# One loop over both halves' queries, and a regrouped top-k selection, in a two-layer decoder trunk on one core

## The chip, the cores and the metric

The kernel runs on one core of a Trainium2 chip. That core has five engines with a program of their own each: TensorE (PE in the rows: matmuls, with PEld for its weight loads), VectorE (DVE), ScalarE (ACT), GpSimd (POOL) and SyncE (SP, which here issues the DMAs). An engine works through its instructions strictly in order and waits on semaphores for the others. The metric is the device time of one execution. Three runs of the kernel before took 2650.87, 2652.57 and 2655.19 us; the median, 2652.57 us, is the time before.

## The reference, cut to what matters

The reference is a decoder trunk of two layers over 1024 tokens of width 1024. The change is in the first layer, a sparse attention. An indexer scores every key for every query; only the 256 best keys of a query are attended to:

```python
dots  = einsum('bqhd,bsd->bqhs', q_idx, k_idx)            # 16 index heads of 64
score = einsum('bqhs,bqh->bqs', relu(dots), w_idx)
score = where(causal, score, -inf)
_, idx = top_k(score, 256)                                 # per query
s = (q_lat . c_sel + q_rope . kr_sel) * 128 ** -0.5        # on the gathered keys
o_lat = softmax(s) @ c_sel
```

Around it lie the projections of the normed input (`h @ w_in`: queries, latent keys, index queries, memory queries), a cross-attention to a memory of 256 rows, and a gated MLP of width 2816 with a causal convolution. The second layer has windowed attention in place of the sparse one. All of it is in float32.

## The kernel before

**Tiling.** Activations lie with features on the 128 partitions and tokens along the free axis, in two halves of 512 tokens. Every float32 product is made of three matmuls on a high and a low part (`mm3`, lines 256 to 258). So each weight block of 128x1024 is split when it is fetched: a load of 512 KB by SP (line 87), a cast on ACT (line 99) and two subtractions of 512 columns on POOL (line 279). Results come out of PSUM by ACT (high part, line 264) and DVE (low part, line 265). PSUM has two buffers of 1024 columns (`pS`) and four of 512 (`pB`).

**Order of the work.** The program is written by hand in one thread. Long pieces of other work are generators; `tick(ns)` advances a virtual clock at each step of the main line, and a background generator issues its next instructions when the nanoseconds that it asked for with `yield` have passed on that clock. So a generator with more yields is spread over more matmuls, and `finish_bg(b)` issues whatever is left of `b` in one piece.

**The stretch concerned.** For each half, `a_q` multiplies the four pairs of query blocks (11 to 18 of `a_in`) with that half's `h`; so each of these eight weight blocks is fetched and split twice. Beside it run in the background the indexer of token blocks 2 to 7 (`indexer`, PE line 1203, ACT line 1206, DVE lines 1209 and 1211), the selection `topk` of blocks 2 and 3 and, once the scores are there, of blocks 4 to 7, and the cross-attention to the memory (`mem_units`, PE lines 713 and 714, DVE line 715, ACT line 719).

**The selection.** A block holds 128 queries; their scores are up to 1024 columns, (block + 1) x 128. `topk` finds the 256th largest score of each row bit by bit: for each of 32 bits it makes a candidate (`cand`), counts how many scores reach it, and keeps the bit or not. DVE counts with line 1239. For the blocks in `act` (6 and 7) ACT counts instead, as a sum of signs of the score less the candidate (line 1247). In one call all blocks go in step: when the last count of a bit is in, lines 1264, 1265 and 1268 judge it for all blocks at once, line 1261 makes the next candidate, line 1244 its negative for ACT, and the first count of the next bit follows with no yield between. For blocks 2 and 3, without `act`, these are lines 1267, 1268 and 1261, then two counts (384 and 512 columns). At the end lines 1291 to 1304 turn the scores into a mask, with the ties resolved; for a block in `act`, lines 1278 to 1287 first find the exact candidate.

**What waits for it.** Attention of the first half starts from `att = self.attn_a(0)`; its unit 2 is the first whose mask needs blocks 2 and 3, and `att[0][2].before` calls `finish_bg(*bt)` for their selection. The selection of blocks 4 to 7 goes on through that attention and through the MLP of the first half. There the down projection fills `pS` with twelve matmuls at a time and DVE adds it to the residual (line 867); a third use of `pS` waits for that add.

Of the kernel before, what the change touches and what calls it, by code (L numbers as in the profile page):

```python
# [173 lines left out]
class Trunk:  # L174
# [970 lines left out]
    def a_q(self, hf, h, tab):  # L1145
        ts = slice(hf * HT, hf * HT + HT)
        for j in (6, 0, 2, 4):
            def dst(hl, e, j=j + 0):
                at = (j + e) * 16
                return self.q_d[hl, at:at + 16].rearrange("i h t -> (i h) t")[:, ts]  # L1150

            S = self.pair("a_in", 11 + j, h)
            if j == 6:
                self.rope_store("q", S, tab, 0, 1.0, dst)
            else:
                self.store_hl("q", S, dst)
# [61 lines left out]
    def topk(self, blks, pace, act=()):  # L1218
# [6 lines left out]

        nc, nb = self.nc, len(blks)
        wks = [self.work[b][:, :(b + 1) * 128] for b in blks]
        ints = self.sb.tile([128, 6, 4], I32, name="ti", tag="ti", bufs=2)
        found, flip, cand, keep, less, pick = [ints[:, i, :nb] for i in range(6)]
        floats = self.sb.tile([128, 5, 4], F32, name="tc", tag="tc", bufs=2)  # L1230
        cnt, need, reach, low, high = [floats[:, i, :nb] for i in range(5)]
        order = [i for i in range(nb) if blks[i] not in act]
        order[1:1] = [i for i in range(nb) if blks[i] in act]
# [8 lines left out]
        def counts():  # L1242
# [10 lines left out]
        for i, b in enumerate(blks):  # L1253
            nc.vector.memset(need[:, i:i + 1], float(2 * TOPK - 1 - (b + 1) * 128 if b in act else TOPK))
        nc.vector.memset(found, 0)
        nc.vector.memset(cand, 0)
        yield from counts()
        nc.vector.tensor_tensor(reach, cnt, need, op=OP.is_lt)
        nc.vector.tensor_scalar(flip, reach, -1.0, 0.0, op0=OP.mult, op1=OP.add)
        for bit in range(30, -1, -1):  # L1260
            nc.vector.scalar_tensor_tensor(cand, found, 1 << bit, flip, op0=OP.bitwise_or, op1=OP.bitwise_xor)
            yield from counts()
            if act:
                nc.vector.tensor_tensor(reach, cnt, need, op=OP.is_ge)
                nc.vector.tensor_scalar(keep, reach, float(1 << bit), 0.0, op0=OP.mult, op1=OP.add)
            else:
                nc.vector.tensor_scalar(keep, cnt, float(TOPK), float(1 << bit), op0=OP.is_ge, op1=OP.mult)
            nc.vector.tensor_tensor(found, found, keep, op=OP.bitwise_or)
        nc.vector.tensor_tensor(cand, found, flip, op=OP.bitwise_xor)
# [431 lines left out]
    def run(self):  # L1701
# [84 lines left out]
        mem = self.mem_units(0)  # L1786
        tab = self.load_table("q32", 0)
# [354 lines left out]
```

## Time and profile before

| of the profiled execution | |
|---|---|
| its time | 2653.03 us |
| span, first to last instruction | 2651.2 us |
| outside the span | 1.8 us |
| median of the three timed runs | 2652.57 us |
| PE busy | 2472.4 us (93%) |
| DVE busy | 1755.7 us (66%) |
| ACT busy | 1188.9 us (45%) |
| POOL busy | 1419.6 us (54%) |
| mean granted TensorE clock | 0.970 of full speed |

A busy time counts the engine as busy while an instruction of it runs, and also while a running instruction is held up; a share over the whole span is a mean over stages with different limits, so the rows further down are of single stretches. The granted clock is 1 at full speed, and half of that in the slow stretches. The selection of blocks 2 and 3 runs from 177 us to 366 us of the span, that of blocks 4 to 7 from 390 us to 857 us.

### The profile page before, as it was taken

What the parts mean: (1) busy time and instruction counts of PE and PEld (TensorE: products, weight loads), DVE (VectorE), ACT (ScalarE), POOL (GpSimd) and SP (SyncE); (2) the same over time, 40 slices, a digit from 0 to 9 for tenths busy, and PEclk for the clock granted to TensorE, in tenths of its full rate; (3) what the DMA queues carried; (4) which work ended last, traced back from release to release, by engine and by line L of the source; (5) the groups of instructions that cost most, each with busy time, mean ns of one, the idle gap of its engine ahead of it and who ended that gap; (6) DMA issues with size and microseconds to landing.
All of it is one profiled execution on the core that took longest, in us unless ns stands there. A gap on an engine that the chain in (4) does not pass through costs nothing. (4 is left out here: it accounts for less than half of the span.)

```text
span 2651.2 us, 34066 instructions
## 1 busy us (share of the span) xinstructions
PE 2472.4 (93%) x11912; PEld 2061.4 (78%) x11912; DVE 1755.7 (66%) x3016; ACT 1188.9 (45%) x2214; POOL 1419.6 (54%) x1256
## 2 busy tenths in 40 slices
PE   7789889989997999999999989999989999999997
PEld 5677668867776889877778878888767888887886
DVE  7899998876779466664663362598786656554446
ACT  5344557644542555433333234678644444441103
POOL 5644344455555643356766655657656565664304
PEclk8899999999998999999999999999999999999999
DMA  5454346422222253332323336543154333348301
GB/s 201 148 172 135 121 135 212 144 72 95 89 80 80 78 189 128 103 106 86 112 81 111 113 84 212 176 159 111 64 182 156 107 112 111 112 160 339 137 23 64
DMA packets 122236, 338.03 MB, mean 127 GB/s; under 512 B 13136, under 2 KB 30032, under 8 KB 122064
## 3 DMA queue, kind: packets, MB, share of 16 engines
q1 hardware_dynamic: 122064, 335.85, 37.5%
q8 instruction: 94, 1.54, 0.2%
q14 instruction: 78, 0.64, 0.1%
HBM read 262.40 MB, written 73.40 MB: 127 GB/s over the span
## 5 line engine op out<-in xcount | busy, mean ns | idle before, releaser
L279 POOL TENSOR_TENSOR t<-t,t 128x512 fp32r<-128x512 f32 (+1 forms) x845 | 1134.1, 1372 | 705.5 <-ACT t L99 274.7
L256 PE MATMUL pB<-t,t 128*128 128x512 f32 (+3 forms) x1824 | 683.1, 374 | 10.6 <-DVE t L781 4.0
L257 PE MATMUL pB<-t,t 128*128 128x512 f32 (+3 forms) x1824 | 679.8, 373 | 9.4 <-DVE t L461 7.4
L258 PE MATMUL pB<-t,t 128*128 128x512 f32 (+3 forms) x1824 | 679.4, 372 | 5.4 <-POOL t L279 5.4
L256 PE MATMUL pS<-t,t 128*128 128x512 f32 (+1 forms) x1460 | 577.1, 395 | 56.4 <-DVE t L867 25.6
L258 PE MATMUL pS<-t,t 128*128 128x512 f32 (+1 forms) x1460 | 571.7, 392 | 9.0 <-POOL t L279 8.8
L257 PE MATMUL pS<-t,t 128*128 128x512 f32 (+1 forms) x1460 | 571.1, 391 | 2.7 <-DVE t L512 2.7
L256 PEld LDWEIGHTS pB<-t,t 128*128 128x128 f32 (+1 forms) x1824 | 346.9, 190 | 71.4 <-DVE t L781 4.8
L257 PEld LDWEIGHTS pB<-t,t 128*128 128x128 f32 (+1 forms) x1824 | 347.0, 190 | 69.3 <-DVE t L461 8.6
L258 PEld LDWEIGHTS pB<-t,t 128*128 128x128 f32 (+1 forms) x1824 | 346.7, 190 | 67.0 <-POOL t L279 6.7
L256 PEld LDWEIGHTS pS<-t,t 128*128 128x128 f32 x1460 | 284.0, 195 | 117.9 <-DVE t L867 35.1
L99 ACT CAST t<-t 128x1024 fp32r<-128x1024 f32 (+1 forms) x292 | 296.9, 1043 | 105.0 <-PE pS L258 49.5
L258 PEld LDWEIGHTS pS<-t,t 128*128 128x128 f32 x1460 | 282.5, 193 | 69.6 <-POOL t L279 13.5
L257 PEld LDWEIGHTS pS<-t,t 128*128 128x128 f32 x1460 | 283.6, 194 | 54.6 <-DVE t L512 3.2
L265 DVE TENSOR_TENSOR t<-pB,t 128x512 fp32r<-128x512 f32 (+3 forms) x248 | 149.7, 622 | 83.4 <-ACT t L264 80.5
L264 ACT CAST t<-pB 128x512 fp32r<-128x512 f32 (+3 forms) x248 | 126.3, 534 | 151.2 <-PE pB L258 88.0
L1055 DVE TENSOR_TENSOR t<-t,pS 128x1024 f32<-128x1024 f32 (+1 forms) x92 | 107.9, 1174 | 125.6 <-PE pS L258 125.4
L867 DVE TENSOR_TENSOR t<-t,pS 128x1024 f32<-128x1024 f32 x88 | 106.4, 1216 | 63.2 <-PE pS L258 63.1
L811 POOL TENSOR_TENSOR t<-t,t 128x512 f32<-128x512 f32 x44 | 57.4, 1304 | 166.8 <-ACT t L810 166.8
L1430 POOL TENSOR_SCALAR t<-t,st 128x128 f32<-128x128 f32 (+3 forms) x64 | 47.8, 749 | 139.5 <-DVE st L1429 79.8
L802 ACT ACTIVATE t<-t,conv 128x512 f32<-128x512 f32 x44 | 35.9, 815 | 171.3 <-DVE t L801 171.3
L1239 DVE TENSOR_SCALAR_CACHE_REDUCE hit<-t,ti 128x384 bf16<-128x384 f32 (+5 forms) x136 | 111.4, 819 | 1.6
(234 smaller groups left out, 3100.1 us busy)
## 6 DMA issues: line engine op xcount, KB each, us to landing
t<-in_up SPq DMA_DIRECT2D x138, 512.0 KB
t<-in_down SPq DMA_DIRECT2D x66, 512.0 KB
G_d<-t SPq DMA_DIRECT2D x44, 512.0 KB
t<-G_d SPq DMA_DIRECT2D x44, 512.0 KB
t<-in_a_in SPq DMA_DIRECT2D x42, 512.0 KB
t<-in_b_in SPq DMA_DIRECT2D x28, 512.0 KB
t<-in_a_out SPq DMA_DIRECT2D x20, 512.0 KB
t<-x_d SPq DMA_DIRECT2D x20, 512.0 KB
```

The costliest lines, as they stand in the source:

```text
L99: nc.scalar.copy(hi[:, :w], raw[:, :w])
L256: mm(out, a[0], b[0], start=start, stop=False, skip_group_check=again)
L257: mm(out, a[0], b[1], start=False, stop=False, skip_group_check=again)
L258: mm(out, a[1], b[0], start=False, stop=stop, skip_group_check=again)
L264: nc.scalar.copy(hi, src)
L265: nc.vector.tensor_tensor(lo, src, hi.bitcast(F32), op=OP.subtract)
L279: self.nc.gpsimd.tensor_tensor(lo[:, s], src[:, s], hi[:, s].bitcast(F32), op=OP.subtract)
L811: nc.gpsimd.tensor_tensor(v, v, rb[0], op=OP.mult)
L867: nc.vector.tensor_tensor(x[dp][:, :, t], x[dp][:, :, t], S, op=OP.add)
L1055: nc.vector.tensor_tensor(xp, xp, S, op=OP.add)
L1239: nc.vector.tensor_scalar(hits("hit")[:, :(blks[i] + 1) * 128], wks[i], cand[:, i:i + 1].bitcast(F32), 0.0, op0=op, op1=OP.add, accum_out= ...
L1430: nc.gpsimd.tensor_scalar(Pt[:, :n], Pt[:, :n], st[:, 2:3], 1.0, op0=OP.mult, op1=OP.mult)
```

## The change

Three things are changed.

First, `a_q` handles both halves in one loop: each pair of query blocks is fetched and split once and multiplied with the first half's `h` and then the second's. The rotation tables are loaded within it, and the memory's cross-attention is put into the background after six of the eight products (`between`), where before it started after four.

Second, the selection of blocks 2 and 3 lets ACT count block 3 (`act=(3,)`).

Third, `topk` keeps no `found`, `flip` and `need` any more: `cand` itself is the number under construction, and one step is two DVE instructions, `drop` (lines 1265 and 1266 of the new file) and the xor into `cand` (line 1267). The step is made apart for the blocks that DVE counts (`own`) and for those that ACT counts, each with a yield behind it; block 6 is counted over 1024 columns, its last 128 filled with -3e38 by POOL.

The two selections get other numbers of yields: a bit of blocks 2 and 3 has three where it had two, a bit of blocks 4 to 7 has four as before.

```diff
-    def a_q(self, hf, h, tab):
+    def a_q(self, hs, between):
+        tabs = [self.load_table("q32", 0)]
         for j in (6, 0, 2, 4):
...
+            us = [self.w.get("a_in", 11 + j + e) for e in range(2)]
+            for hf, h in enumerate(hs):
...
+                for e in range(2):
+                    self.proj(S[:, e], us[e], h)
...
+            if j == 2:
+                between()
...
         def count(i, op):
             nc.vector.tensor_scalar(hits("hit")[:, :(blks[i] + 1) * 128], wks[i], cand[:, i:i + 1].bitcast(F32), 0.0,
                                     op0=op, op1=OP.add, accum_out=cnt[:, i:i + 1])
...
+        def step(bit, part):
+            at, need = part
+            nc.vector.tensor_scalar(drop[:, at], cnt[:, at], float(need), float(1 << bit) if bit < 31 else -1.0,
+                                    op0=OP.is_lt, op1=OP.mult)
+            nc.vector.scalar_tensor_tensor(cand[:, at], drop[:, at], 1 << bit >> 1, cand[:, at],
+                                           op0=OP.bitwise_xor, op1=OP.bitwise_xor)
+
+        for bit in range(31, -1, -1):
+            for k in range(max(len(own), nb - len(own))):
+                if len(own) + k < nb:
+                    i = len(own) + k
+                    nc.scalar.activation(hits("sign")[:, :wide], self.work[blks[i]][:, :wide], AF.Sign,
+                                         bias=cand[:, i:i + 1].bitcast(F32), accum_out=cnt[:, i:i + 1])
+                if k < len(own):
+                    count(k, OP.is_ge)
+                yield pace
+            if own:
+                step(bit, parts[0])
+                yield pace
             if act:
-                nc.vector.tensor_scalar(less, cand, -(1 << 31), None, op0=OP.bitwise_xor)
-            for i in order:
-                if blks[i] in act:
-                    nc.scalar.activation(hits("sign")[:, :(blks[i] + 1) * 128], wks[i], AF.Sign,
-                                         bias=less[:, i:i + 1].bitcast(F32), accum_out=cnt[:, i:i + 1])
-                else:
-                    count(i, OP.is_ge)
+                step(bit, parts[-1])
                 yield pace
...
-        for bit in range(30, -1, -1):
-            nc.vector.scalar_tensor_tensor(cand, found, 1 << bit, flip, op0=OP.bitwise_or, op1=OP.bitwise_xor)
-            yield from counts()
-            if act:
-                nc.vector.tensor_tensor(reach, cnt, need, op=OP.is_ge)
-                nc.vector.tensor_scalar(keep, reach, float(1 << bit), 0.0, op0=OP.mult, op1=OP.add)
-            else:
-                nc.vector.tensor_scalar(keep, cnt, float(TOPK), float(1 << bit), op0=OP.is_ge, op1=OP.mult)
-            nc.vector.tensor_tensor(found, found, keep, op=OP.bitwise_or)
...
-            bt.append(self.add_bg(self.topk((2, 3), 1400)))
+            bt.append(self.add_bg(self.topk((2, 3), 1400, (3,))))
...
-        self.a_q(0, h0, tab)
-        tab = self.load_table("q32", 1)
         bgs.append(self.a_latent(1, h1))
-        bm = self.add_bg(self.whole(mem[0]))
-        self.a_q(1, h1, tab)
+        reads = []
+        self.a_q((h0, h1), lambda: reads.append(self.add_bg(self.whole(mem[0]))))
+        bm = reads[0]
```

By the built programs the change takes away 8 DMAs of `in_a_in` on SP, 8 casts of 128x1024 on ACT and 16 subtractions of 128x512 on POOL, and 31 counts of 512 columns on DVE; it adds 32 counts of 512 columns on ACT and turns 32 of 896 columns into 1024. PE's instructions are the same in number.

What moves is seen in two places. The first is DVE in the MLP's down projection of the first half; L867 is the add to the residual, L1264 to L1244 judge one bit of blocks 4 to 7 and make the next candidate, L1239 counts. Before:

```order
L1264 TENSOR_TENSOR tc<-tc 128x4
L1265 TENSOR_SCALAR ti<-tc 128x4
L1268 TENSOR_TENSOR ti<-ti 128x4
L1261 SCALAR_TENSOR_TENSOR ti<-ti 128x4
L1244 TENSOR_SCALAR ti<-ti 128x4
L1239 TENSOR_SCALAR hit,tc<-t_1918,ti 128x640
L867 TENSOR_TENSOR t_3731<-t_3731,pS 128x1024
L867 TENSOR_TENSOR t_3733<-t_3733,pS 128x1024
```

And now, with L1265 and L1267 the two instructions of a step and L1254 the count:

```order
L867 TENSOR_TENSOR t_3567<-t_3567,pS 128x1024
L1265 TENSOR_SCALAR ti<-tc 128x2
L1267 SCALAR_TENSOR_TENSOR ti<-ti 128x2
L1254 TENSOR_SCALAR hit,tc<-t_1911,ti 128x640
L867 TENSOR_TENSOR t_3569<-t_3569,pS 128x1024
L1254 TENSOR_SCALAR hit,tc<-t_2285,ti 128x768
L867 TENSOR_TENSOR t_3571<-t_3571,pS 128x1024
L1265 TENSOR_SCALAR ti<-tc 128x2
L1267 SCALAR_TENSOR_TENSOR ti<-ti 128x2
L867 TENSOR_TENSOR t_3573<-t_3573,pS 128x1024
```

Where six instructions of the selection stood in one run ahead of an add, runs of one to three now stand between the adds.

The second place is DVE just ahead of attention unit 2 of the first half; L620 and L622 take the second half's memory queries out of PSUM, L265 is the next evacuation that PE needs, and t_1134 and t_1323 are the scores of blocks 2 and 3. Before:

```order
L1244 TENSOR_SCALAR ti<-ti 128x4
L1239 TENSOR_SCALAR hit,tc<-t_1918,ti 128x640
L620 SCALAR_TENSOR_TENSOR t_3723<-pS,t_3723 64x1024
L622 SCALAR_TENSOR_TENSOR t_3724<-pS,t_3724 64x1024
L265 TENSOR_TENSOR t_3743<-pB,t_3743 128x384
L1421 ISA t_3750,st<-pB,t_1134 128x384
```

And now, first the beginning and then the end of what stands between L622 and L265:

```order
L620 SCALAR_TENSOR_TENSOR t_3561<-pS,t_3561 64x1024
L622 SCALAR_TENSOR_TENSOR t_3562<-pS,t_3562 64x1024
L1265 TENSOR_SCALAR ti<-tc 128x1
L1267 SCALAR_TENSOR_TENSOR ti<-ti 128x1
L1254 TENSOR_SCALAR hit,tc<-t_1134,ti 128x384
L1265 TENSOR_SCALAR ti<-tc 128x1
L1267 SCALAR_TENSOR_TENSOR ti<-ti 128x1
```

```order
L1304 TENSOR_TENSOR ti<-ti,tc 128x1
L1254 TENSOR_SCALAR hit,tc<-t_1323,ti 128x512
L1308 TENSOR_SCALAR tc<-tc 128x2
L1313 TENSOR_SCALAR t_3626<-t_1134,ti 128x384
L1315 SCALAR_TENSOR_TENSOR t_3627<-t_3626 128x384
L1317 SCALAR_TENSOR_TENSOR t_3627<-t_3627,tc,t_3626 128x384
L1319 SCALAR_TENSOR_TENSOR t_1134<-t_1134,ti,t_3627 128x384
L1321 TENSOR_SCALAR t_1134<-t_1134 128x384
```

The selection of blocks 2 and 3, which had ended well ahead of this place, is now unfinished there: its last four bits and all that follows them, 47 instructions of DVE and 4 counts of ACT, are issued in one piece between L622 and L265.

## Rows read from the trace of the kernel before

**Rows 1.** Page, part 1: busy us (share of the span) xinstructions, by engine.
```profile
PE 2472.4 (93%) x11912; PEld 2061.4 (78%) x11912; DVE 1755.7 (66%) x3016; ACT 1188.9 (45%) x2214; POOL 1419.6 (54%) x1256
```
**Rows 2.** Busy time by stretch: PE, PEld, DVE, ACT, POOL; clock, DMA share, GB/s.
```profile
165.00:400.00 235.00, 208.83 (x991) 170.79 (x990) 214.13 (x402) 118.83 (x232) 105.03 (x80) 0.96 0.42 138
425.00:550.00 125.00, 117.37 (x650) 100.10 (x649) 103.40 (x264) 75.84 (x158) 55.13 (x57) 0.97 0.45 149
550.00:800.00 250.00, 230.39 (x979) 187.62 (x978) 176.35 (x290) 119.88 (x188) 137.68 (x108) 0.97 0.25 83
```
**Rows 3.** Waits, 165 to 400 us: who for whom, us in total, times, longest.
```profile
PE pB L1203 <- ACT t L719: 13.7, 4, 8.6
...
ACT t L719 <- DVE st L715: 21.3, 6, 9.3
```
**Rows 4.** Waits of PE, 550 to 800 us.
```profile
PE pS L256 <- DVE t L867: 18.0, 6, 6.9
```
**Rows 5.** Timeline of PE: start us, us, instruction, [idle before, releaser].
```profile
599.13 0.79 PE L256 MATMUL pS<-t,t 128*128 128x512 f32 x1 [6.92 <-DVE t L867]
...
603.13 0.63 PE L256 MATMUL pS<-t,t 128*128 128x512 f32 x1
...
604.11 0.39 PE L256 MATMUL pS<-t,t 128*128 128x512 f32 x1
```
**Rows 6.** Timeline of DVE, and POOL beside it, at 668 us.
```profile
668.88 0.15 DVE L1264 TENSOR_TENSOR tc<-tc 128x4 f32<-128x4 f32 x1
669.07 1.17 DVE L1265 TENSOR_SCALAR ti<-tc 128x4 int32<-128x4 f32 x1
...
672.74 1.19 DVE L1244 TENSOR_SCALAR ti<-ti 128x4 int32<-128x4 int32 x1
673.84 0.87 DVE L1239 TENSOR_SCALAR_CACHE_REDUCE hit<-t,ti 128x640 bf16<-128x640 f32 x1
...
667.69 6.21 POOL L279 TENSOR_TENSOR t<-t,t 128x512 fp32r<-128x512 f32 x5 [1.51 <-ACT t L820]
```
**Rows 7.** Groups of DVE by form, selection of blocks 2 and 3: busy us, mean ns.
```profile
L1239 DVE TENSOR_SCALAR_CACHE_REDUCE hit<-t,ti 128x512 bf16<-128x512 f32 x33 | 24.4, 741 | 0.3
L1239 DVE TENSOR_SCALAR_CACHE_REDUCE hit<-t,ti 128x384 bf16<-128x384 f32 x33 | 20.2, 612 | 1.2
L1267 DVE TENSOR_SCALAR ti<-tc 128x2 int32<-128x2 f32 x31 | 18.0, 582 | 0.2
L1268 DVE TENSOR_TENSOR ti<-ti 128x2 int32<-128x2 int32 x31 | 12.4, 400 | 1.1
L1261 DVE SCALAR_TENSOR_TENSOR ti<-ti 128x2 int32<-128x2 int32 x31 | 8.1, 262 | 1.1
```
**Rows 8.** Groups of DVE, 338 to 380 us: the masks of blocks 2 and 3.
```profile
L1302 DVE SCALAR_TENSOR_TENSOR t<-t,ti,t 128x384 f32<-128x384 f32 (+1 forms) x2 | 2.3, 1140 | 0.1
L1298 DVE TENSOR_TENSOR_SCAN t<-t 128x384 f32<-128x384 f32 (+1 forms) x2 | 2.3, 1140 | 0.1
L1304 DVE TENSOR_SCALAR t<-t 128x384 f32<-128x384 f32 (+1 forms) x2 | 1.8, 876 | 0.0
L1300 DVE SCALAR_TENSOR_TENSOR t<-t,tc,t 128x384 f32<-128x384 f32 (+1 forms) x2 | 1.6, 790 | 0.0
L1296 DVE TENSOR_SCALAR t<-t,ti 128x384 f32<-128x384 f32 (+1 forms) x2 | 1.1, 525 | 0.0
```
**Rows 9.** Groups: ACT's count over 1024 columns, and POOL's splits from 165 to 400 us.
```profile
L1247 ACT ACTIVATE sign<-t,ti 128x1024 bf16<-128x1024 f32 x32 | 36.7, 1147 | 0.5
...
L279 POOL TENSOR_TENSOR t<-t,t 128x512 fp32r<-128x512 f32 (+2 forms) x62 | 88.7, 1454 | 115.6 <-ACT t L99 83.2 <-issue 22.2 <-DMA q_d<-t 7.3
```
**Rows 10.** Timelines of DVE and PE at attention unit 2, before.
```profile
405.34 0.17 DVE L1258 TENSOR_TENSOR tc<-tc 128x4 f32<-128x4 f32 x1
405.54 0.17 DVE L1259 TENSOR_SCALAR ti<-tc 128x4 int32<-128x4 f32 x1
...
411.08 0.96 PE L1417 MATMUL pB<-t,t 128*128 128x512 f32 x3 [3.50 <-DVE t L265]
```

More of the change, by code (lines that the diff above doesn't have):

```diff
@@ L1143, in a_latent, with dst @@
         return self.add_bg(latent_norm())
-    def a_q(self, hf, h, tab):
-        ts = slice(hf * HT, hf * HT + HT)
+    def a_q(self, hs, between):
+        tabs = [self.load_table("q32", 0)]
         for j in (6, 0, 2, 4):
[L1148 to L1154, printed above, removed]
-            else:
-                self.store_hl("q", S, dst)
+            us = [self.w.get("a_in", 11 + j + e) for e in range(2)]
+            for hf, h in enumerate(hs):
+                ts = slice(hf * HT, hf * HT + HT)
+                def dst(hl, e, j=j + 0, ts=ts):
+                    at = (j + e) * 16
+                    return self.q_d[hl, at:at + 16].rearrange("i h t -> (i h) t")[:, ts]
+                S = self.psS().rearrange("p (j t) -> p j t", j=2)
+                for e in range(2):
+                    self.proj(S[:, e], us[e], h)
+                if j == 6:
+                    self.rope_store("q", S, tabs[hf], 0, 1.0, dst)
+                    if not hf:
+                        tabs.append(self.load_table("q32", 1))
+                else:
+                    self.store_hl("q", S, dst)
+            if j == 2:
+                between()
     def a_first(self, raw, rb):
@@ L1226, in topk @@
         nc, nb = self.nc, len(blks)
+        own = [b for b in blks if b not in act]
+        blks = own + [b for b in blks if b in act]
         wks = [self.work[b][:, :(b + 1) * 128] for b in blks]
[L1228 to L1233, printed above, removed]
+        ints = self.sb.tile([128, 3, 4], I32, name="ti", tag="ti", bufs=2)
+        cand, drop, pick = [ints[:, i, :nb] for i in range(3)]
+        floats = self.sb.tile([128, 3, 4], F32, name="tc", tag="tc", bufs=2)
+        cnt, low, high = [floats[:, i, :nb] for i in range(3)]
+        wide = (max(act) + 1) * 128 if act else 0
+        parts = [(slice(0, len(own)), TOPK), (slice(len(own), nb), 2 * TOPK - 1 - wide)]
         def hits(tag):
@@ L1240, in count @@
                                     op0=op, op1=OP.add, accum_out=cnt[:, i:i + 1])
-        def counts():
-            if act:
-                nc.vector.tensor_scalar(less, cand, -(1 << 31), None, op0=OP.bitwise_xor)
-            for i in order:
-                if blks[i] in act:
-                    nc.scalar.activation(hits("sign")[:, :(blks[i] + 1) * 128], wks[i], AF.Sign,
-                                         bias=less[:, i:i + 1].bitcast(F32), accum_out=cnt[:, i:i + 1])
-                else:
-                    count(i, OP.is_ge)
-                yield pace
@@ L1253, in topk @@
[L1253 to L1256, printed above, removed]
-        yield from counts()
-        nc.vector.tensor_tensor(reach, cnt, need, op=OP.is_lt)
-        nc.vector.tensor_scalar(flip, reach, -1.0, 0.0, op0=OP.mult, op1=OP.add)
-        for bit in range(30, -1, -1):
-            nc.vector.scalar_tensor_tensor(cand, found, 1 << bit, flip, op0=OP.bitwise_or, op1=OP.bitwise_xor)
-            yield from counts()
-            if act:
-                nc.vector.tensor_tensor(reach, cnt, need, op=OP.is_ge)
-                nc.vector.tensor_scalar(keep, reach, float(1 << bit), 0.0, op0=OP.mult, op1=OP.add)
-            else:
-                nc.vector.tensor_scalar(keep, cnt, float(TOPK), float(1 << bit), op0=OP.is_ge, op1=OP.mult)
-            nc.vector.tensor_tensor(found, found, keep, op=OP.bitwise_or)
@@ L1269, in topk @@
-        nc.vector.tensor_tensor(cand, found, flip, op=OP.bitwise_xor)
+        nc.vector.memset(cand, 0)
+        if act:
+            nc.vector.tensor_scalar(cand[:, len(own):], cand[:, len(own):], -(1 << 31), None, op0=OP.bitwise_xor)
+            for b in act:
+                if (b + 1) * 128 < wide:
+                    nc.gpsimd.memset(self.work[b][:, (b + 1) * 128:wide], -3e38)
+        def step(bit, part):
[4 more added lines that the diff above has]
+                                           op0=OP.bitwise_xor, op1=OP.bitwise_xor)
@@ L1270, in topk @@
+        if act:
+            nc.vector.tensor_scalar(cand[:, len(own):], cand[:, len(own):], -(1 << 31), None, op0=OP.bitwise_xor)
         for i in range(nb):
@@ L1786, in run @@
         mem = self.mem_units(0)
-        tab = self.load_table("q32", 0)
         bgs.append(self.a_latent(1, h1))
-        self.a_q(0, h0, tab)
-        tab = self.load_table("q32", 1)
+        reads = []
+        self.a_q((h0, h1), lambda: reads.append(self.add_bg(self.whole(mem[0]))))
+        bm = reads[0]
         del h0
-        bm = self.add_bg(self.whole(mem[0]))
-        self.a_q(1, h1, tab)
         self.finish_bg(*bgs, be)
@@ L1800, in run @@
         self.store_qmem(self.pair("a_in", 19, h1), 1)
-        del h1, tab
+        del h1
         self.finish_bg(ba)
```

## The prediction, made before the changed kernel had run

> **What bounds the kernel now.** The first view is the page's part 1 [rows 1]: PE is busy 93% of the span, DVE 66%, ACT 45%, POOL 54%. So PE is the bound on the mean, and a change on the other engines can win only what PE loses by waiting for them, or by running at half clock after a wait. The second view is the busy time by stretch [rows 2], to see where that loss lies within the reach of the change. From 165 to 400 us PE is busy 208.83 of 235 us, so it idles 26.2 us; the mean granted clock is 0.96, and 4% of 235 us, 9.4 us, is what the slow clock took. DVE is busy 214.13 us there, 91%, more than PE. From 425 to 550 us (attention) the loss is 7.6 us idle and 3.8 us of clock, from 550 to 800 us (the MLP) 19.6 us and 7.5 us. After the selection's end at 857 us, no instruction is changed.
>
> The third view is who waits for whom. From 165 to 400 us the largest entry has PE waiting 13.7 us for ACT's L719, but ACT's L719 itself waits 21.3 us for DVE's L715 [rows 3]: the late engine is DVE. From 550 to 800 us 18.0 of PE's 19.6 us are six waits for L867, DVE's add to the residual [rows 4]. The timeline shows what such a wait costs in all: after 6.92 us of waiting PE runs its matmuls 0.63 us long until past 603 us, at half of full clock, and 0.39 us long from 604.11 us on [rows 5]. And it shows why DVE is late: at 668.88 us it judges a bit, and four of the five small instructions, on 4 elements per partition, take some 1.2 us each; then a count of 0.87 us follows, and only then an add. POOL is working through five splits from 667.69 us for 6.21 us [rows 6], so the small ones end where POOL's end.
>
> **The change part by part.** All sums are made against the profiled execution: 2653.03 us, of which 2651.2 us are the span. That is 0.5 us above the median of the runs shown.
>
> *Fetching the query weights once.* 8 loads of 512 KB, 8 casts and 16 subtractions go. DMA is busy 42% there and POOL 105.03 of 235 us [rows 2], so neither is on the path, and the direct gain is nothing. Indirectly, 16 x 1.45 us [rows 9] = 23 us of POOL's 105 go, and with them a fifth of the occasions on which DVE is held up; that is in the middle value below.
>
> *Blocks 2 and 3, ahead of attention unit 2.* DVE loses 31 counts of 512 columns: 31 x 0.741 = 23.0 us [rows 7]. A bit had three small instructions and now has four (two steps of two). Those three take 0.582, 0.400 and 0.262 us on the mean [rows 7], 0.415 us each; at that price the 93 before cost 38.6 us. Of the 128 now, 18 lie in the piece ahead of unit 2, and 110 cost 45.6 us: 7.0 us more. The dearest price, 0.582 us for each, gives 25 us more; with 0.17 us, that of an unhindered one [rows 10], it is 20 us less. With three yields per bit in place of two the selection is slower by the virtual clock, and four bits, the last counts and the masks fall out of this stretch: 4 x 0.612, 0.612 + 0.741 and the masks' 2.3 + 2.3 + 1.8 + 1.6 + 1.1 = 9.1 us [rows 7, 8], together 12.9 us. So DVE has 214.1 - 23.0 + 7.0 - 12.9 = 185 us of work ahead of unit 2. PE needs 235 - 35.6 = 199 us without any loss. DVE falls below PE and the backlog can drain. ACT gets 28 counts of 512 columns, each below the 1.147 us of 1024 columns [rows 9]: at most 32 us on 118.83 of 235 [rows 2], room enough.
>
> How much of the 35.6 us comes back no row says directly. The nearest is 425 to 550 us, where DVE is busy 83% and PE loses 11.4 of 125 us, 9% [rows 2]; at that rate 199 us of work take 219 us, a gain of 16. If half the loss goes, the stretch takes 209 us, a gain of 26. I take 20 us. The bounds: nothing (the dearest small instructions put DVE at 203 us, over PE's 199, and ACT's counts now stand in line behind DVE), and 35 us.
>
> *The piece ahead of unit 2.* DVE runs in order, and L265, which empties the PSUM buffer that PE needs next, stands behind the piece. Its length: 24 small instructions at the 0.20 us from start to start of [rows 10] = 4.8 us; 5 counts of 384 columns, 3.1 us; 2 of 512, 1.5 us; for the exact candidate of block 3 two selections at the 0.525 us of L1296 and two reductions, for which the nearest row is the count of the same width, 0.741 us, 2.5 us; the masks 9.1 us [rows 7, 8]. Together 21 us. ACT's four counts run beside DVE's own, and hardly add. PE has two or three microseconds of scores and transposes that need nothing from the piece. The same place costs a wait of 3.50 us already [rows 10], and the piece comes on top: 20 us. After it PE starts at half clock, as in [rows 5]; 6 us of that lose 3 us. So 23 us lost. The bounds are 14 us (the masks at their cheapest, and more of PE's work found ahead) and 45 us (every small instruction at 1.2 us, as in [rows 6]).
>
> Here a rule of the Trainium skill weighs in: SBUF — State Buffer, section SBUF: two separate sides, has it that VectorE and GpSimd share one pair of ports as an exclusive lock, taken for a whole instruction by whichever starts first, and that a VectorE instruction with two SBUF inputs needs the pair. By that, the small ones in the piece cost 0.2 us, since POOL has little left to do when PE stands, where the mean row of 0.415 us would make the piece 5 us longer. The trace agrees where it can: in [rows 6] the small ones stretch as long as POOL's splits run.
>
> *Blocks 4 to 7, in attention and the MLP.* A bit had five small instructions and the first count in one run; now it has two pairs with yields between, and at most a pair and a count meet: 2 x 1.2 + 0.87 us at worst against 4 x 1.2 + 0.87 us in [rows 6]. Two buffers of `pS` give DVE the time of twelve matmuls per add, so most of the six waits go. ACT's count of block 6 grows from 896 to 1024 columns, 0.1 us each, hidden by its idle half. I take 20 us of the 27.1 us lost between 550 and 800 us (15 of the 18.0 us waited for L867, and 5 of the 7.5 us of clock). The bounds are 5 us (the pairs still meet an add badly) and 27 us. In attention PE hardly waits for these steps: 2 us, between 0 and 6. The rest of the MLP, 800 to 900 us, has the masks of blocks 4 to 7 in the same order as before: nothing.
>
> The sum: -20 + 23 - 20 - 2 = -19 us. 2653.03 - 19 = 2634 us.
>
> **The rivals.** *All of the backlog goes.* For it: DVE's 185 us against PE's 199. Against: bursts remain, as in every stretch of [rows 2]. 30 us gained ahead of unit 2, 18 lost at the piece, 25 and 4 gained after: 2612 us.
>
> *ACT is tied to DVE.* Before, ACT evacuated the indexer's scores whether or not DVE's selection was late. Now a count of ACT stands ahead of these evacuations and waits for DVE's step of the same bit. For it: DVE is late ahead of unit 2 [rows 3]. Against: the step is issued a yield earlier. If that eats the 20 us, the sum is +1: 2654 us.
>
> *The waits for L867 stay.* If they come from POOL's splits more than from the length of the run, one pair held up twice is enough: 5 gained in place of 20, a sum of -4: 2649 us. Against: four held instructions made the run of [rows 6], and two are the most now.
>
> *The piece ahead of unit 2 decides: slower.* Its price is that of DVE in order, with PE behind it. If POOL still has splits and the memory's scalings in that time, and the small ones cost 1.2 us, the piece is 45 us; with 3 us of clock, and 16 gained ahead, 17 after and 1 in attention, the sum is +14: 2667 us. It decides from about 42 us on, what the other terms give together. Against: PE stands, so POOL runs dry.
>
> **How the numbers follow.** My forecast, 2622 to 2646 us, has a chance of 0.58; all of the backlog 0.14; ACT tied to DVE 0.11; the waits stay 0.07; the piece decides 0.10. Faster or slower means by over 0.2% of the median, below 2647.3 or above 2657.9 us, about what a measurement can tell. Faster: 0.58 + 0.14 and a third of the two middle rivals, together 0.76. Same: most of the rest of these, 0.13. Slower: 0.11. The range from 2611 to 2656 us takes in both sides up to the two middle rivals, and leaves out the slower one and the far end of the faster.
>
> **What would show each step.** Right: from 165 us to unit 2, DVE's busy share falls below PE's, and PE's wait for L719 shrinks; one wait of PE of some 20 us stands ahead of unit 2, released by L265 on DVE; between 550 and 800 us waits for L867 come to under 5 us, and the clock there is 0.99. Wrong: DVE still at 90% or more ahead of unit 2; ACT waiting long for the selection's steps with PE behind it; no wait of over 10 us at unit 2; or six waits for L867 as before. The whole is wrong if the time lies above 2656 us.

## The result and the profile after

The changed kernel takes 2624.34 us (median of four runs, 2623.16 to 2625.82) against 2653.77 us before: ratio 0.9885, 95% interval 0.9871 to 0.9900, so 29.4 us faster. The forecast was 19 us. Page of the changed kernel, part 1 (answers [rows 1]):

```profile
PE 2457.8 (94%) x11912; PEld 2053.0 (78%) x11912; DVE 1708.0 (65%) x2961; ACT 1207.9 (46%) x2270; POOL 1387.8 (53%) x1241
```

The same stretches as [rows 2], in the changed kernel:

```profile
165.00:400.00 235.00, 206.96 (x1005) 170.82 (x1003) 183.56 (x388) 138.83 (x293) 78.83 (x69) 0.95 0.43 143
425.00:550.00 125.00, 119.23 (x658) 102.35 (x659) 102.70 (x243) 76.41 (x156) 54.24 (x55) 0.97 0.43 141
550.00:800.00 250.00, 242.90 (x1051) 199.35 (x1050) 187.51 (x297) 127.30 (x194) 157.50 (x122) 0.98 0.26 86
```

From 165 to 400 us PE is no busier than before, 206.96 against 208.83 us, because its long wait at unit 2 lies in this stretch now. Up to that wait, from 165 to 377.8 us, PE is busy 206.93 us and DVE 163.05 us, where 185 us of work for DVE ahead of unit 2 were forecast. From 550 to 800 us PE gained 12.5 us of busy time. Waits of PE in the changed kernel, first from 370 to 430 us, then from 550 to 800 us (answers [rows 4]):

```profile
PE pB L713 <- DVE t L265: 22.8, 1, 22.8
...
PE pS L256 <- DVE ti L1301: 3.9, 1, 3.9
PE pS L256 <- DVE t L867: 3.2, 2, 2.5
```

The 22.8 us are, but for some 3 us in front of it, the piece ahead of unit 2. The 18.0 us for L867 have become 3.2. Nothing is left either of PE's wait in [rows 3]: from 165 to 375 us PE waits nowhere for L719. The piece on DVE, from its first step to the evacuation behind it:

```profile
380.78 0.15 DVE L1265 TENSOR_SCALAR ti<-tc 128x1 int32<-128x1 f32 x1
380.97 0.16 DVE L1267 SCALAR_TENSOR_TENSOR ti<-ti 128x1 int32<-128x1 int32 x1
381.05 0.60 DVE L1254 TENSOR_SCALAR_CACHE_REDUCE hit<-t,ti 128x384 bf16<-128x384 f32 x1
...
388.96 1.36 DVE L1295 TENSOR_SCALAR t<-t,ti 128x512 f32<-128x512 f32 x1
390.35 1.36 DVE L1297 CUSTOM_DVE_ANT_0 t<-t,t 128x512 f32<-128x512 f32 x1
...
399.60 0.43 DVE L1321 TENSOR_SCALAR t<-t 128x512 f32<-128x512 f32 x1
400.05 0.56 DVE L265 TENSOR_TENSOR t<-pB,t 128x384 fp32r<-128x384 f32 x1
```

It is 19.3 us long (21 forecast). Its small instructions take 0.15 and 0.16 us. Two long ones, L1295 and L1297, take 1.36 us each, where the same lines took 0.48 and 0.69 us just before (387.70 and 388.22 us); they stand beside POOL's only two splits of this time (388.23 us, 2.93 us). PE in the same place:

```profile
400.67 0.58 PE L713 MATMUL pB<-t,t 128*128 128x256 f32 x1 [22.83 <-DVE t L265]
...
401.04 0.42 PE L714 MATMUL pB<-t,t 128*128 128x256 f32 x1
...
405.17 0.28 PE L256 MATMUL pB<-t,t 128*128 128x256 f32 x1
```

At 401 us a matmul of 256 columns takes 0.42 us, at 405 us 0.28: some 4 us after the wait run at half of full clock (the granted clock is half until 404.4 us), as in [rows 5].

The kernels issue the same number of matmuls, and outside `a_q` and what is mixed with it in the same order. So the trace also tells when PE starts the n-th one in it, and how far that is ahead of before. All figures are worked out from one profiled execution of each kernel. Up to matmul 490 (138.3 us before), where the selection has not begun, these already differ by up to 4 us, and behind the MLP's end, where the last masks alone are left of the selection, by up to 5 us more. The last column is a difference within one execution, so free of the first of these. From matmul 1121 to 1716 the new `a_q` has another order: at matmul 1396 it has 4096 columns more behind it than before, at 1577 7680, which at 0.23 us for 512 columns (from start to start in before, at full clock) are an estimated 1.8 and 3.4 us of work. In these two columns, then, the runs with the new `a_q` are best compared with one another; before, e6 and e7 have the old order. The names are those of the experiments below.

| gain on before, us | ahead of unit 2 (matmul 1396, 357.8 us) | behind its wait (1577, 401.1 us) | attention's end (2361, 553.3 us) | MLP's end (3381, 819.2 us) | length of the MLP, 2361 to 3381 (265.9 before) |
|---|---|---|---|---|---|
| changed kernel | 20.5 | -1.1 | 1.7 | 27.3 | 240.3 |
| e1, no piece | 10.2 | 3.9 | 7.0 | 32.6 | 240.3 |
| e4, no piece, DVE counts | 14.9 | 12.8 | 15.6 | 41.2 | 240.3 |
| e2, weights once alone | 9.5 | 9.4 | 10.8 | 8.4 | 268.3 |
| e12, loop alone | 1.5 | 0.0 | 1.3 | -0.8 | 268.1 |
| e3, joined steps | 16.6 | -7.5 | -12.5 | 10.1 | 243.3 |
| e5, joined, longer | 20.5 | -3.7 | -8.2 | 8.2 | 249.5 |
| e9, count before steps | 21.3 | -2.9 | -7.6 | 4.2 | 254.1 |
| e6, before, shifted | -1.3 | 0.3 | -3.6 | 1.2 | 261.1 |
| e7, before, short splits | 13.9 | 17.3 | 19.5 | 27.8 | 257.5 |
| e11, best | 27.2 | 19.5 | 24.8 | 57.0 | 233.7 |

By the first row the 28.8 us between the two profiled executions (2653.03 and 2624.22 us) are: 20.5 won ahead of unit 2 and 2.7 more on the way to the piece; 24.3 lost at it; 2.8 won in attention; 25.6 in the MLP; 1.5 after it. Of the 2.8 in attention some belong to the new order: with before's selection e12 and e2 have 1.3 and 1.4 there.

### The profile page after: what moved, and what is told of

Its sections match the earlier page's. It is cut to its first block, busy times and chain, and to the rows that moved or that the text cites. A ratio compares the mean times of both kernels' runs of the same rounds, so it can differ in the third digit from the quotient of the medians.

```text
span 2622.4 us, 34006 instructions
## 1 busy us (share of the span) xinstructions
PE 2457.8 (94%) x11912; PEld 2053.0 (78%) x11912; DVE 1708.0 (65%) x2961; ACT 1207.9 (46%) x2270; POOL 1387.8 (53%) x1241
## 5 line engine op out<-in xcount | busy, mean ns | idle before, releaser
L279 POOL TENSOR_TENSOR t<-t,t 128x512 fp32r<-128x512 f32 x829 | 1108.2, 1368 | 681.0 <-ACT t L99 273.6
L256 PEld LDWEIGHTS pS<-t,t 128*128 128x128 f32 x1460 | 281.7, 193 | 100.4 <-ACT t L99 22.8
L99 ACT CAST t<-t 128x1024 fp32r<-128x1024 f32 x284 | 288.0, 1043 | 101.5 <-PE pS L258 44.1
L265 DVE TENSOR_TENSOR t<-pB,t 128x512 fp32r<-128x512 f32 (+3 forms) x248 | 149.8, 623 | 85.3 <-ACT t L264 82.7
L811 POOL TENSOR_TENSOR t<-t,t 128x512 f32<-128x512 f32 x44 | 57.5, 1306 | 161.6 <-ACT t L810 161.6
L867 DVE TENSOR_TENSOR t<-t,pS 128x1024 f32<-128x1024 f32 x88 | 106.8, 1217 | 53.0 <-PE pS L258 52.7
L1274 ACT ACTIVATE sign<-t,ti 128x1024 bf16<-128x1024 f32 (+1 forms) x96 | 96.5, 1005 | 60.5 <-DVE ti L1267 49.1
L1222 DVE SCALAR_TENSOR_TENSOR t<-t,wtok,t 128x384 f32<-128x384 f32 (+5 forms) x90 | 97.0, 1077 | 24.5 <-ACT t L1217 20.7
```

Of the source, the lines that this page charges most:

```text
L99: nc.scalar.copy(hi[:, :w], raw[:, :w])
L256: mm(out, a[0], b[0], start=start, stop=False, skip_group_check=again)
L265: nc.vector.tensor_tensor(lo, src, hi.bitcast(F32), op=OP.subtract)
L279: self.nc.gpsimd.tensor_tensor(lo[:, s], src[:, s], hi[:, s].bitcast(F32), op=OP.subtract)
L811: nc.gpsimd.tensor_tensor(v, v, rb[0], op=OP.mult)
L867: nc.vector.tensor_tensor(x[dp][:, :, t], x[dp][:, :, t], S, op=OP.add)
```

## The experiments

**e1, no piece.** The selection of blocks 2 and 3 is spread as before's was, so nothing is left of it at unit 2.

```diff
-            bt.append(self.add_bg(self.topk((2, 3), 1400, (3,))))
+            bt.append(self.add_bg(self.topk((2, 3), 950, (3,))))
```

> The changed kernel with one number changed: the selection of blocks 2 and 3 asks for 950 ns per yield in place of 1400, so three yields a bit take as long on the virtual clock as before's two, and the whole selection is issued ahead of unit 2; nothing is left to issue in one piece. Theory A (the 20 us won ahead of unit 2 come from fewer DVE instructions: 31 counts of 512 columns gone): the wait of 22.8 us for L265 falls to about 3 us, the gain ahead of unit 2 stays at 15 us or more, and the time is 2602 to 2612 us. Rival B (the 20 us were won because work was put off into the piece): DVE gets about 13 us of work back ahead of unit 2, that stretch gives back what the piece cost, and the time stays at 2619 to 2627 us.

Measured: 2624.83 us (ratio 0.9886, 0.9868 to 0.9904), the same as the changed kernel. The wait of 22.8 us is 3.4, but the gain ahead of unit 2 is 10.2 us in place of 20.5. So rival B: half of that gain was work put off, which the piece gave back. Waits of ACT in e1, 165 to 375 us, then those of PE:

```profile
ACT sign L1274 <- DVE ti L1267: 44.7, 27, 3.7
...
PE pB L1214 <- ACT t L1217: 8.5, 13, 2.1
```

L1274 is ACT's count, L1267 the step that makes its candidate. In the changed kernel the same two are 18.6 us, 12 times, and 2.7 us. Since ACT takes its instructions in order, the indexer's evacuations (L1217) stand behind a count that waits for DVE, and PE can stand behind them. What that costs is the question of e4.

**e4, no piece, DVE counts block 3.**

```diff
-            bt.append(self.add_bg(self.topk((2, 3), 950, (3,))))
+            bt.append(self.add_bg(self.topk((2, 3), 950)))
```

> As the run without the piece (950 ns per yield), but block 3 is counted on DVE as before: 33 counts of 512 columns are DVE's again, and ACT's counts go. Theory A (block 3's counts on ACT are what takes DVE below PE ahead of unit 2): 23 us of DVE's work come back, and the time lies 10 to 22 us above that run. Rival B (the shorter step, the yields or the weights fetched once do it): within 4 us of that run.

Measured: 2615.43 us (0.9850, 0.9836 to 0.9863), 9.4 us below e1, where theory A had it 10 to 22 us above. Theory A has fallen: counting block 3 on ACT costs 9 us here, together with the step of its own that such a block needs (e1 has four small instructions a bit, e4 two). The stretch from 165 to 375 us, in e1 and then in e4:

```profile
165.00:375.00 210.00, 194.92 (x921) 157.80 (x919) 169.59 (x361) 122.67 (x257) 67.45 (x54) 0.98 0.40 128
```

```profile
165.00:375.00 210.00, 198.02 (x958) 163.57 (x957) 187.91 (x353) 107.66 (x210) 71.62 (x57) 0.99 0.40 132
```

With 18.3 us more of DVE's busy time PE does 37 matmuls more. PE's largest wait in e4, same stretch:

```profile
PE pB L1214 <- ACT t L1217: 7.0, 9, 3.1
```

In all PE waits 12.9 us in e1, all of it for ACT (3.8 us for the cast L99), and 12.0 us in e4, 8.0 for ACT and 4.0 for DVE. So the waits for ACT are 4.9 us longer in e1, those for DVE shorter, and the mean clock of e1 is a little lower. That the queue of ACT is the way by which the 9 us are lost fits, but these rows don't add up to it: it is argued, not shown.

**e2, weights fetched once.** Before, with the changed `a_q` alone.

```diff
-            S = self.pair("a_in", 11 + j, h)
+            us = [self.w.get("a_in", 11 + j + e) for e in range(2)]
+            for hf, h in enumerate(hs):
...
+                for e in range(2):
+                    self.proj(S[:, e], us[e], h)
```

> The kernel before with the query projection of the changed one alone (one loop over both halves, weights fetched and split once, memory units started after six of the eight products); the selection is before's. Theory A (that part is worth nothing by itself, DVE's selection keeps the stretch late): 2646 to 2655 us, with PE still losing about 30 us from 165 to 400 us. Rival B (POOL's 16 splits less and the later memory units are what lets the backlog drain): 2630 to 2640 us, with 12 us or more won ahead of unit 2.

Measured: 2645.13 us (0.9955, 0.9941 to 0.9969), between the two: the part whose direct gain I put at nothing is worth 10 us. DVE's small instructions of blocks 2 and 3 in e2, by form (answers to the last three of [rows 7]):

```profile
L1278 DVE TENSOR_SCALAR ti<-tc 128x2 int32<-128x2 f32 x31 | 11.4, 369 | 0.2
L1272 DVE SCALAR_TENSOR_TENSOR ti<-ti 128x2 int32<-128x2 int32 x31 | 8.2, 265 | 1.1
L1279 DVE TENSOR_TENSOR ti<-ti 128x2 int32<-128x2 int32 x31 | 8.1, 262 | 1.1
```

Together 27.7 us, where [rows 7] has 38.5. Two runs ask what does that.

**e10, the memory's start.**

```diff
-            if j == 2:
+            if j == 0:
                 between()
```

> The query projection of the changed kernel alone, as in the run with weights fetched once, but the memory's cross-attention starts after four of the eight products, as in before, in place of six. Theory A (the 10 us of that run came from the memory units' later start: they met DVE's backlog where it was deepest, with PE behind L719): 2650 to 2656 us, and PE waits 8 us or more for L719 from 165 to 400 us. Rival B (they came from POOL's 16 splits less): 2641 to 2648 us, with waits for L719 under 5 us.

Measured: 2644.86 us (0.9967, 0.9956 to 0.9979), with 0.9 us waited for L719: rival B, the memory units' later start is not it.

**e12, the loop alone.**

```diff
-            us = [self.w.get("a_in", 11 + j + e) for e in range(2)]
             for hf, h in enumerate(hs):
+                us = [self.w.get("a_in", 11 + j + e) for e in range(2)]
```

> The kernel before with the changed query projection's loop over both halves, but each weight block fetched and split anew for the second half, so that loads, casts and POOL's subtractions are as many as in before; memory units after six of the eight products. In the run with weights fetched once, the three small instructions per bit of blocks 2 and 3 fell from 38.5 to 27.7 us in all, and the time by 10 us. Theory B (the 16 splits of POOL less are what shortens DVE's small instructions, and that is the gain): the three are at 34 us or more again, and the time is 2649 to 2656 us. Rival D (the order of the loop is what gains): 2641 to 2647 us, and the three stay below 31 us.

Measured: 2654.30 us (1.0006, 0.9996 to 1.0016), the same as before. The small instructions in e12:

```profile
L1278 DVE TENSOR_SCALAR ti<-tc 128x2 int32<-128x2 f32 x31 | 14.0, 451 | 0.2
L1279 DVE TENSOR_TENSOR ti<-ti 128x2 int32<-128x2 int32 x31 | 13.4, 432 | 1.1
L1272 DVE SCALAR_TENSOR_TENSOR ti<-ti 128x2 int32<-128x2 int32 x31 | 11.3, 365 | 1.1
```

38.7 us, as before. So fetching once is the gain. That it is the 16 splits among what goes with a fetch (a load, a cast, two splits) shows in the small instructions: of the 93, 23 took over 0.3 us before, 13 in e2 and 23 in e12, and every one of these started while a subtraction of POOL ran, or at most 0.15 us before one began (165 to 375 us). PE waits 8.7 us for ACT in e2 (7.2 for L1217, 1.5 for L719) and 15.3 in e12 (12.8 and 2.5).

**e3, joined steps.** In the changed kernel both steps of a bit of blocks 4 to 7 are issued in one run again, with the next count right behind.

```diff
+            joint = nb == 4
+            if joint:
+                yield 2 * pace
             if own:
                 step(bit, parts[0])
-                yield pace
+                if not joint:
+                    yield pace
             if act:
                 step(bit, parts[-1])
-                yield pace
+                if not joint:
+                    yield pace
```

> The changed kernel with the two steps of a bit of blocks 4 to 7 joined in one run that the next count follows with no yield between; the yields that are taken out are added ahead of it, so a bit lasts as long on the virtual clock and the instructions are the same in number and shape. Theory A (the length of the run that stands ahead of an add L867 makes PE wait): about half or more of the 24 us won from 550 to 800 us is lost, several waits for L867 come back (8 us or more in all), and the time is 2634 to 2648 us. Rival B (the win came from four small instructions per bit in place of five, or from the lower count of them alone): the time stays at 2622 to 2630 us, and waits for L867 stay at about 3 us.

Measured: 2642.06 us (0.9947, 0.9933 to 0.9961), the time of theory A but not by its way. In the MLP the waits for L867 are 4.2 us, and the MLP lasts 243.3 us where the changed kernel has 240.3. It is 17.7 us above the changed kernel by the medians; the profiled execution is the slowest of its five, 21.4 us above. Of these 21.4 the table has 7.8 in attention (e3 loses 5.0 us from matmul 1577 to 2361, the changed kernel gains 2.8), 3.0 in the MLP, and 6.4 up to matmul 1577: 2.6 of them stand at matmul 490 already, and 2.6 are a longer wait at unit 2 (25.4 us). The last 4.2 come behind the MLP. So pairs in place of one run are worth 3 us in the MLP, not 20. Why are e3's runs harmless? Before, DVE and then POOL:

```profile
566.66 0.69 DVE L816 TENSOR_TENSOR t<-t,pB 128x512 f32<-128x512 f32 x1 [0.47 <-POOL t L811]
567.26 1.01 DVE L1239 TENSOR_SCALAR_CACHE_REDUCE hit<-t,ti 128x768 bf16<-128x768 f32 x1
...
568.38 0.16 DVE L1264 TENSOR_TENSOR tc<-tc 128x4 f32<-128x4 f32 x1
568.58 1.18 DVE L1265 TENSOR_SCALAR ti<-tc 128x4 int32<-128x4 f32 x1
...
565.33 1.30 POOL L811 TENSOR_TENSOR t<-t,t 128x512 f32<-128x512 f32 x1 [1.35 <-ACT t L810]
568.43 6.31 POOL L279 TENSOR_TENSOR t<-t,t 128x512 fp32r<-128x512 f32 x5 [1.81 <-ACT t L820]
```

And e3, at another bit:

```profile
589.32 0.69 DVE L816 TENSOR_TENSOR t<-t,pB 128x512 f32<-128x512 f32 x1 [1.22 <-POOL t L811]
589.92 0.16 DVE L1265 TENSOR_SCALAR ti<-tc 128x2 int32<-128x2 f32 x1
...
590.39 0.16 DVE L1267 SCALAR_TENSOR_TENSOR ti<-ti 128x2 int32<-128x2 int32 x1
...
587.98 1.31 POOL L811 TENSOR_TENSOR t<-t,t 128x512 f32<-128x512 f32 x1 [1.35 <-ACT t L810]
590.74 6.75 POOL L279 TENSOR_TENSOR t<-t,t 128x512 fp32r<-128x512 f32 x5 [1.46 <-ACT t L820]
```

DVE goes on (L816) when POOL's L811 ends, and between L811 and the next splits POOL pauses for 1.5 to 1.8 us, waiting for ACT's L820. Before, the count of 768 columns fills that pause and the run meets the splits; in e3 that count came two yields earlier and the run fits in. Of 22 runs of small instructions in the MLP 13 took over 1.3 us before, 4 in e3.

**e9, count before steps.** e3 with that count put back.

```diff
+                if nb == 4 and k == 1:
+                    yield 2 * pace
                 if k < len(own):
                     count(k, OP.is_ge)
                 yield pace
             joint = nb == 4
-            if joint:
-                yield 2 * pace
```

> The joined steps of blocks 4 to 7 once more (four small instructions in a run), with only the count of 768 columns moved: it stands one yield ahead of the run, where the kernel before has it, in place of three yields. In the run with joined steps, 4 of 22 runs between 555 and 820 us took over 1.3 us; in before 13 of 22. Theory C (in before this count of 1.01 us pushes the run past the 1.45 us between POOL's L811 and its splits, into the splits): 9 or more of 22 runs take over 1.3 us again, waits for L867 from 550 to 800 us are 8 us or more in place of 4.2 us, and the time is 2646 to 2658 us. Rival D (five instructions, or the wait of before's first one for ACT's counts, is what made them late): at most 6 of 22, waits under 6 us, 2638 to 2646 us.

Measured: 2650.30 us (0.9991, 0.9981 to 1.0000); 14 of 22 runs over 1.3 us; the MLP lasts 254.1 us, 10.8 more than in e3; the waits for L867 are 7.9 us by 800 us, a hair under the 8 expected, and 12.0 by the MLP's end. Theory C holds for the runs and for some 11 us of the MLP.

**e5, joined and longer.** e3 with two more small instructions in the run.

```diff
+                if joint:
+                    for _ in range(2):
+                        nc.vector.scalar_tensor_tensor(pick[:, :2], drop[:, :2], 1 << bit >> 1, drop[:, 2:4],
+                                                       op0=OP.bitwise_xor, op1=OP.bitwise_xor)
```

> The joined steps of the run before (both steps of a bit of blocks 4 to 7 in one run, followed by the next count with no yield), with two more small instructions on 128x2 elements in that run, whose results nothing uses: six small instructions where the joined run has four. The joined run left PE waiting only 4.2 us for L867 from 550 to 800 us, where before's five small instructions, in the same place, left 18.0 us. Theory A (the length of the run that is held up beside POOL's splits decides, with a threshold between about 3 us, where PE hardly waits, and 5 us, where it waits 7 us): waits for L867 of 9 us or more, and 8 to 25 us above the joined run's 2642 us. Rival B (the place of the run against POOL's splits decides, not its length): waits stay under 6 us, and the time within 5 us of the joined run's.

Measured: 2647.50 us (0.9978, 0.9969 to 0.9987); waits for L867 7.9 us; the MLP 249.5 us. That is 5.4 us above e3 by the medians (some 8 by the ratios, since before was faster in this round) and 6.2 us in the MLP: between the two. Length counts, but six instructions that mostly meet the pause (4 of 22 runs over 1.3 us) do less harm than before's five that mostly don't.

**e6, before, shifted by half a pace.**

```diff
+        if nb == 4:
+            yield 1200
         ints = self.sb.tile([128, 6, 4], I32, name="ti", tag="ti", bufs=2)
```

> The kernel before with the selection of blocks 4 to 7 begun 1200 ns of the virtual clock later (one more yield at its start), half of the 2400 ns between its steps; no instruction changes. Theory A (length of the run: five small instructions and a count in line): the runs still meet POOL's splits about as often, so waits for L867 from 550 to 800 us are 11 to 25 us in all, and the time 2645 to 2662 us. Rival B (the place of the runs against splits and adds decides): the waits fall to under 8 us, and the time to 2633 to 2643 us.

Measured: 2649.76 us (0.9986, 0.9976 to 0.9997), with four waits for L867 of 19.8 us in all, and 14 of 22 runs over 1.3 us: theory A. A shift of all steps at once moves the waits and doesn't remove them.

**e7, before, short splits.**

```diff
-    PIECE = 512
+    PIECE = 256
```

> The kernel before with POOL's subtractions done in pieces of 256 columns in place of 512, everywhere: twice the instructions on POOL, each about half as long. Theory A (a small instruction of DVE beside them waits for one of POOL's to end): the small ones of 1.2 us fall to 0.6 to 0.8 us, the run ahead of an add halves, waits for L867 from 550 to 800 us fall below 8 us; the time is 2625 to 2648 us if POOL's longer sums cost nothing elsewhere. Rival B (1.2 us is the price of a small instruction after a count or on int32, whatever POOL does): they stay at 1.2 us, and the waits at 14 us or more.

Measured: 2619.98 us (0.9873, 0.9855 to 0.9891), 34 us faster, as much as the whole change. POOL from 550 to 800 us, and the dearest small instruction of [rows 7] from 165 to 400 us, in e7:

```profile
L279 POOL TENSOR_TENSOR t<-t,t 128x256 fp32r<-128x256 f32 x201 | 152.7, 802 | 59.1 <-ACT t L820 31.5 <-issue 21.0 <-ACT t L99 3.6
...
L1267 DVE TENSOR_SCALAR ti<-tc 128x2 int32<-128x2 f32 x31 | 13.1, 423 | 0.2
```

Splits of 0.80 us hold a small instruction for less long (the mean of L1267 fell from 0.582 to 0.423 us), but they hold more of them: of the 93 small instructions of [rows 7] 40 took over 0.3 us, where before had 23, and the three lines together still take 35.4 us of 38.5. In the MLP 14 of 20 runs took over 1.3 us, and the waits for L867 are still 16.7 us. The table has 17.3 us won up to unit 2, 2.7 of them by matmul 490, and 8.4 in the MLP. So the time is shown, but not by which wait it came; the small instructions that were looked at explain little of it. Theory A's time was too cautious and its waits too few.

**e8 and e11, the best.** e8 is e4 with 1050 ns per yield, and e11 is e8 with e7's edit as well.

```diff
-            bt.append(self.add_bg(self.topk((2, 3), 950)))
+            bt.append(self.add_bg(self.topk((2, 3), 1050)))
...
-    PIECE = 512
+    PIECE = 256
```

> The version with block 3 counted on DVE, with 1050 ns per yield in place of 950: the selection is spread further and still wholly issued ahead of unit 2. Theory A (a thinner selection gives PE less to wait for ahead of unit 2, with nothing paid at unit 2): 3 to 8 us below the 2615 us of that version. Rival B (no room is left, or the masks now stand close enough ahead of unit 2 to hold up L265): within 3 us of it, or above.

> The version with block 3 counted on DVE at 1050 ns per yield, with POOL's subtractions in pieces of 256 columns everywhere. Alone, the first gave 41 us on before, the second 34 us. Theory A (both save partly the same, what small instructions of DVE wait beside POOL's splits): 2592 to 2606 us. Rival B (they save the same wholly): 2607 to 2614 us. Rival C (twice the instructions on POOL cost as much as they give once the steps are short): above 2614 us.

Measured: e8 2612.49 us (0.9848, 0.9830 to 0.9866), not told apart from e4, with 5.3 us waited for L265 ahead of unit 2. e11 2589.53 us (0.9758, 0.9745 to 0.9771): 63 us faster than before and 35 us below the changed kernel's time, a little below theory A's range. Its wait for L867:

```profile
PE pS L256 <- DVE t L867: 1.8, 1, 1.8
```

## Why the prediction was right, and where it wasn't

The time lay in the range, and each of the four terms of the sum had the right sign and nearly its size; but two of them were reached in part by a wrong reason, and the two large ones ahead of unit 2 and at it belong together and cancel.

- *Weights fetched once, 0.* Mis-sized: 10 us alone (e2), and the loop without the fetching gives nothing (e12). The step had named the way, a fifth of POOL's occasions to hold up DVE, and then left it inside another term without a price.
- *Ahead of unit 2, -20.* Measured -20.5. That DVE falls below PE came true (163.05 against 206.93 us up to PE's wait), and by more than forecast: the small instructions there took 0.27 us on the mean (29.7 us for 112 of them, 165 to 375 us), not 0.415. But how far DVE lies below PE does not set the gain, and "room enough" for ACT failed: e4 gives DVE more work than e1 and is 9 us faster. Step by step the 20.5 us are: 1.5 from the loop (e12), 8.0 from fetching once (e2 less e12), 5.4 from the shorter step and its yields (e4 less e2), 4.7 lost by counting on ACT (e1 less e4), and 10.3 from work put off (changed less e1). A chain of differences adds up by itself, and each carries the scatter of single executions.
- *The rival that ACT is tied to DVE*, with a chance of 0.11, named what fits best here, with the wrong end: counting on ACT costs 9 us by e1 and e4, not the whole 20, and it didn't decide the time.
- *The piece, +23.* Measured +24.3, with 19.3 us of DVE and a wait of 22.8. The wait is longer than the piece, and than the 20 us forecast, since PE stopped at 377.84 us, 2.9 us ahead of the piece, while L620 and L622 still stood before it; the forecast had PE work two or three microseconds into it. The small instructions took 0.15 and 0.16 us there, and L1295 beside POOL's splits 1.36: this is what the Trainium skill (SBUF — State Buffer, section SBUF: two separate sides) has of the shared ports, and the trace agrees. But the term and the postponement in the one before belong together: without both the time is the same (e1).
- *Attention, -2.* Measured -2.8, of which some 1.4 come with the new order of `a_q` (e2 and e12). By e3 this was no small matter: joined runs lose 8 us there against the changed kernel.
- *The MLP, -20.* Measured -25.6, the largest error of size. The waits for L867 fell by 15.5 us from matmul 2361 to 3381 (15 forecast), and the clock gave back an estimated 6, worked out from the granted clock outside the waits (5 forecast). What the term left out are 3.0 us of other waits: 1.6 for a split of POOL, which are gone, and 1.4 at the end of the selection (before, PE waits 5.3 us for L1284 at 812.9 us, now 3.9 for L1301). The step that failed is "at most a pair and a count meet", as the cause: going from the changed kernel back to before, pairs are worth 3.0 us (e3 against the changed kernel) and the count's place 10.8 (e9 against e3). The remaining 11.8 (before against e9) go with four small instructions for five and a step that needs not all of ACT's counts at once (before, L1264 waits 6.4 us in all for L1247 from 550 to 800 us). These two were not told apart; e5 puts two instructions at 6.2 us. In another order of taking them away the shares could differ.
- *After 800 us, nothing.* 1.5 us, within the scatter of single executions.

That the total came 10 us better than forecast is the MLP (5.6), the last 2.7 us ahead of the piece, and the small rest. One sum of the prediction is off: 0.58 + 0.14 and a third of 0.11 + 0.07 make 0.78 for faster, not 0.76.

## What to carry to other kernels

Before you move work to an engine with room, look at what its queue holds behind the new instruction: an in-order engine that waits for another passes that wait on to everything behind it. Here the move cost 9 us, and that this is the way fits but is not shown. Where a small instruction takes seven times its own time, look for the long one on the neighbouring engine; cutting that one in halves was worth as much here (e7) as all three changes, though by which waits is open. A gain ahead of a point at which postponed work falls due is not a gain until that point is passed.

## What the runs showed of the hardware

Which of DVE's instructions POOL holds up was finer than I had it. From 165 to 400 us of the changed kernel 66 times L1265, all but two on one element per partition, took 134 to 268 ns; L1267 beside it went up to 1151 ns. It is not that L1265 missed the splits: 17 of the one-element ones started while one ran, and none took over 156 ns; of the 16 of L1267 that did, 15 took 480 ns or more. On 128x2 elements, in the MLP, L1265 too goes up to 1240 ns. The counts are never stretched: 609 ns at most for 384 columns beside POOL's subtractions, against a mean of 612 in [rows 7]. The Trainium skill fits for all but the first: SBUF — State Buffer, section Who interferes with whom, names among those that need the shared ports a `tensor_scalar`, but not the form that also writes its accumulator (the counts), and any instruction with two SBUF inputs (L1267). The Trainium skill, VectorE: DVE Perf Modes, section Mode 2×_2P, asks of the first for an even count, or for an odd one that is equal in source and destination; one element is not ruled out by that, so why it escapes here stays open.

What a hold costs is the rest of one POOL instruction: up to some 1.2 us beside splits of 512 columns, mostly 0.64 to 0.67 us beside those of 256 (L1268 and L1261 in e7). A single-input instruction on one element per partition was not held here, and POOL's work in shorter pieces shortened the time; no term of the prediction had either.
